# Attention products of two heads on the two halves of TensorE, with results kept feature-major

## The chip, the cores and the metric

One core of a Trainium2 chip runs the whole kernel in one launch. The metric is the device time in microseconds. The engines are TensorE (PE: matrix products; PEld its weight loads), VectorE (DVE), ScalarE (ACT), GpSimd (POOL) and SyncE (SP), whose queue issues nearly all weight transfers. Products land in PSUM, eight banks of 128 x 512 fp32; everything else lives in SBUF.

## What is computed

A chain of transformer blocks on 256 tokens of width 1024, all in fp32. The first block is a gated feed-forward, a mixer (window attention with a context of 256 tokens beside a bidirectional gated scan) and a second feed-forward. A second block follows, twice over, with four token mixers, a gated merge and a mixture of 32 experts. Cut to what the change touches:

```python
s_band = jnp.einsum('bkgnqd,bknsd->bkgnqs', qb, kb).astype(jnp.float32) * scale
...
p = softmax_with_sink(jnp.concatenate([s_band, s_ctx], axis=-1), sink_b).astype(v.dtype)
o = (jnp.einsum('bkgnqs,bknsd->bkgnqd', p[..., :3 * BLOCK], vb)
     + jnp.einsum('bkgnqs,bksd->bkgnqd', p[..., 3 * BLOCK:], vc))
...
o_a = mla_attention(q_nope, q_rope, k_nope, k_rope, v_a).reshape(b, s_len, A_WIDTH)
o_b = stick_breaking_attention(sb[:, :, 0], sb[:, :, 1], sb[:, :, 2]).reshape(b, s_len, B_WIDTH)
o_c = sliding_window_attention(...).reshape(b, s_len, C_WIDTH)
o_d = (rms_norm(o, subln) * (1.0 - lam_init)).reshape(b, s_len, D_WIDTH)
gates = jax.nn.sigmoid(jnp.einsum('bsd,de->bse', x, w_gate) + b_gate).reshape(b, s_len, N_BRANCH, D_MODEL)
merged = (gates[:, :, 0] * jnp.einsum('bsw,wd->bsd', o_a, w_br_a) + ...)
return jnp.einsum('bsd,de->bse', merged, w_out)
```

Heads are 64 wide (differential: scores 32 wide, values 64): eight query heads over two key/value heads in window and sliding-window attention, four heads in the other three.

## The kernel before

Dense products keep fp32 accuracy with three matmuls in fp32r: weights and activations are each cut into a high and a low part, and `mm3` (L149 to L152) adds high x high, high x low and low x high. `Weights` streams 128 x 1024 weight units in a fixed sequence: SP loads a unit into a raw slot, ACT writes the high part (L96), DVE the low part (L97), and a product takes it (`feature_major`, `token_major`). Attention products are plain fp32 matmuls; each stands in the trace as two passes with two records.

PSUM is one pool with two tags of four banks each (`pmm`): "mm" for dense products and "ax" for everything else. Which instruction comes when on each engine is settled when the kernel is built: a scheduler places the instructions of the program in an order on every engine, bound by the buffers that the tiles hold. Tiles of one tag are handed out in program order; a tile gets a buffer when the tile that had it is done with. In the layers all longer-lived tiles share one tag, "u", with 13 buffers (`unit`, L1128):

```python
    def unit(shape, name, dt=FT):
        return U.tile([128] + list(shape), dt, name=name, tag="u", bufs=SHARED)
```

**First block.** `attention(i)` (L825 to L861), for each of two blocks of 128 queries and each of eight heads: scores (L833, one matmul 128 x 512 on 64 rows of the array), mask (L836), maximum (L838 to L840), exp with its sum (L842), four transposes of the probabilities (L845), copy (L847 or L143), four PV products with the probabilities as weights and 64 columns of V streaming (L849), so that the result is token-major; then the division by the sum and four transposes of the result (`rows_T`, L818). It is a generator that yields once per head; `within(i)` is the scan's (L875, L876, L899). L917 to L922 run nine steps of the one with three steps of the other in between. Dense products of the next stage are placed between them by the scheduler.

**A layer** (loop at L1134): projections; sliding-window attention (scores L1254, bias L1257, softmax, transposes L1206, PV L1268); differential attention (scores L1292, bias L1295, maximum L1217, exp L1224, combination L1299 to L1304, PV L1311); stick-breaking (scores L1335 and L1336, L1338 and L1340 on DVE, exp L1341, ln L1342, L1343, suffix products L1345 to L1348, L1349, exp L1350, PV L1356). Exp and ln are in different tables of ACT, and a change of table is an ACT_TABLE_LOAD. Then MLA attention (units `mq`, `mk`; scores L1409, PV L1416) and the gates (32 dense products of 24 matmuls each, for eight units `gt`; tanh at L1428). All five results are token-major, in `OT`, 1280 columns wide; 20 transposes (L1451) turn them into five units `oT` for the merge with the branch weights (L1470 on). Router and experts follow (L1658, L1686); their weights, 192 loads of 512 KB a layer, stream into slots that come free with the attention part.

Of the kernel before, what the change touches and what calls it, by code (L numbers as in the profile page):

```python
# [24 lines left out]
ETB = 2  # L25
QUADS = 8
# [94 lines left out]
def build(tc, A, out):  # L121
# [202 lines left out]
    def gate_rows(pool, i, r, w):  # L324
# [6 lines left out]
        return G  # L331

# [802 lines left out]
    for l in range(2):  # L1135
# [10 lines left out]
        OT = [pL.tile([128, 1280], FT, name=f"o{i}") for i in range(2)]  # L1146
# [93 lines left out]
        project("swk", 1)  # L1240
        for i in range(2):
# [3 lines left out]

            PO = pmm("ax")
            den = pa.tile([128, 8], FT, name="den", bufs=3)
            for s in range(2):
                for g0 in range(0, 4, per):
                    P = pmm("ax")  # L1250
                    Pv = P.rearrange("p (a b) -> p a b", a=per)
                    sc = pa.tile([128, 512], FT, name="sc", bufs=2).rearrange("p (a b) -> p a b", a=per)
                    for j in range(per):
                        PE.matmul(Pv[:, j, :], lhsT=qs["swq"][64 * s:64 * s + 64, g0 + j, qsl],  # L1254
                                  rhs=qs["swk"][64 * s:64 * s + 64, 0, :keys], start=True, stop=True)
                    for j in range(per):
                        V.scalar_tensor_tensor(sc[:, j, :], dist[:, 1, 128 * i:128 * i + keys], -sw_slopes[4 * s + g0 + j],  # L1257
                                               Pv[:, j, :], op0=OP.mult, op1=OP.add)
# [724 lines left out]
```

## Time and profile before

| | |
|---|---|
| median of 3 runs | 2079.13 us (2071.57 to 2079.62) |
| the profiled execution | 2080.24 us, its span 2078.3 us |
| mean granted clock of TensorE | 0.969 |
| PE busy | 1887.0 us, 91% of the span |
| DVE, ACT, POOL busy | 1099.0, 791.3, 244.3 us |
| DMA | 436.61 MB, mean 210 GB/s |

The profile has the share of each engine on one page, and views of the trace give busy time by stretch, by line, and each instruction in order of time. In the timelines "x8" means that eight records in a row were put together; the time given is from the first's start to the last's end, and since matmuls are pipelined, what one costs is read from the start of a row to the start of the next.

### The profile page before, as it was taken

To read this page: it belongs to the slowest core of one execution; us is meant where nothing else is said; L and a number is where in the kernel's file an instruction comes from. 1 tells how busy PE (TensorE), PEld (TensorE's weight loads), DVE (VectorE), ACT (ScalarE), POOL (GpSimd) and SP (SyncE) were. 2 spreads that over 40 slices of the span, in tenths; PEclk is the share of its full clock that TensorE was granted. 3 is DMA by queue.
4 is the path that set the end of the run, shared out by engine and by line. 5 is a ranking of instruction groups with operands and counts; after the bars stand their busy time and mean duration, and the time that the engine had idled before them with its cause. 6 is when DMAs were issued, how large, how long until landed. Compare 5 with 4: busy or idle time off the path is not lost. (4 is left out here: it accounts for less than half of the span.)

```text
span 2078.3 us, 29398 instructions
## 1 busy us (share of the span) xinstructions
PE 1887.0 (91%) x11414; PEld 1447.1 (70%) x11414; DVE 1099.0 (53%) x2083; ACT 791.3 (38%) x1365; POOL 244.3 (12%) x172
## 2 busy tenths in 40 slices
PE   6979999989999897999999997978869999988886
PEld 2757788877778787998888996533238899853331
DVE  4775465484656567554668556211147864641122
ACT  3443222453444444444445644211035465331111
POOL 2653000131131220000100011000020000200000
PEclk9999999999999998999999999999989999989999
DMA  8543575442242134556434378889954445879897
GB/s 317 193 142 122 181 239 198 151 151 87 73 134 81 62 125 131 186 190 191 137 115 138 123 261 313 338 350 412 413 203 133 131 132 177 320 293 412 351 412 283
DMA packets 120118, 436.61 MB, mean 210 GB/s; under 512 B 13616, under 2 KB 13664, under 8 KB 119968
## 3 DMA queue, kind: packets, MB, share of 16 engines
q1 hardware_dynamic: 116208, 422.63, 56.6%
q0 software_dynamic: 2608, 8.32, 1.3%
q10 hardware_dynamic: 1152, 3.67, 0.5%
q8 instruction: 94, 1.54, 0.3%
q14 instruction: 56, 0.46, 0.1%
HBM read 433.51 MB, written 1.05 MB: 209 GB/s over the span
## 5 line engine op out<-in xcount | busy, mean ns | idle before, releaser
L1658 PE MATMUL ax<-raw,xg 128*32 128x512 f32 x1024 | 179.5, 597 | 9.5 <-DMA raw<-in_moe 9.5
L97 DVE TENSOR_TENSOR split7l<-raw,split7h 128x1024 fp32r<-128x1024 f32 x98 | 126.6, 1292 | 112.7 <-ACT split7h L96 112.5
L97 DVE TENSOR_TENSOR split6l<-raw,split6h 128x1024 fp32r<-128x1024 f32 x99 | 128.4, 1297 | 84.4 <-ACT split6h L96 81.5
L96 ACT ACTIVATE split7h<-raw 128x1024 fp32r<-128x1024 f32 x101 | 106.8, 1057 | 169.4 <-PE mm L152 67.0
L96 ACT ACTIVATE split6h<-raw 128x1024 fp32r<-128x1024 f32 x102 | 107.9, 1058 | 161.6 <-issue 59.2
L1658 PEld LDWEIGHTS ax<-raw,xg 128*32 128x32 f32 x1024 | 39.1, 109 | 111.5 <-issue 59.6
L1460 POOL DMA_DIRECT2D gb<-in_lnrows x8 | 4.4, 549 | 835.9 <-DMA raw<-in_moe 416.2
L1686 PE MATMUL ax<-raw,ehT 128*32 128x512 f32 x512 | 87.0, 599 | 15.0 <-ACT ehT L143 12.7
L584 DVE SCALAR_TENSOR_TENSOR xn<-raw,xn 128x1024 f32<-128x1024 f32 x56 | 85.0, 1517 | 23.3 <-DMA raw<-in_w_mod 22.6
L1629 PEld LDWEIGHTS ax<-OH,X 128*128 128x128 f32 x512 | 69.4, 217 | 36.5 <-issue 32.2
L1629 PE MATMUL ax<-OH,X 128*128 128x128 f32 x512 | 75.1, 307 | 13.3 <-issue 11.2
L1691 DVE SCALAR_TENSOR_TENSOR yl<-ax,gsl,yh 128x512 fp32r<-128x512 f32 x32 | 24.0, 751 | 116.1 <-ACT yh L1690 111.7
L581 POOL TENSOR_TENSOR raw<-raw,xn 128x1024 f32<-128x1024 f32 x24 | 72.5, 3030 | 74.8 <-DVE xn L584 56.8
L1667 DVE TENSOR_TENSOR ehs<-ax,ehs 128x256 f32<-128x256 f32 x16 | 6.8, 425 | 119.4 <-ACT ehs L1666 119.4
L361 ACT ACTIVATE xg<-ax,cols 128x128 f32<-128x128 f32 x64 | 24.0, 456 | 117.8 <-PE ax L1629 117.8
L1686 PEld LDWEIGHTS ax<-raw,ehT 128*32 128x32 f32 x512 | 19.3, 108 | 65.4 <-issue 27.6
L1666 ACT ACTIVATE ehs<-ax 128x256 f32<-128x256 f32 x16 | 6.1, 383 | 151.4 <-PE ax L1658 151.4
L363 DVE TENSOR_SCALAR xg<-ax,cols 128x128 f32<-128x128 f32 x64 | 21.9, 405 | 78.0 <-PE ax L1629 78.0
L150 PE MATMUL mm<-hThi,split6h 128*128 128x512 f32 x128 | 52.5, 410 | 6.2 <-ACT split6h L96 4.2
L1690 ACT ACTIVATE yh<-ax,gsl 128x512 fp32r<-128x512 f32 x32 | 21.9, 686 | 94.5 <-PE ax L1686 94.5
L152 PE MATMUL mm<-hThi,split6l 128*128 128x512 f32 x128 | 52.5, 410 | 5.3 <-DVE split6l L97 5.3
L152 PE MATMUL mm<-hxhi,split7l 128*128 128x256 f32 x192 | 54.5, 284 | 2.0 <-POOL split7l L97 1.2
(876 smaller groups left out, 5856.7 us busy)
## 6 DMA issues: line engine op xcount, KB each, us to landing
raw<-in_moe SPq DMA_DIRECT2D x384, 512.0 KB, 10.1
raw<-in_f_in SPq DMA_DIRECT2D x88, 512.0 KB, 4.3
raw<-in_w_gate SPq DMA_DIRECT2D x64, 512.0 KB, 3.5
raw<-in_w_mod SPq DMA_DIRECT2D x56, 512.0 KB, 4.3
raw<-in_f_out SPq DMA_DIRECT2D x55, 512.0 KB, 4.2
raw<-in_w_out SPq DMA_DIRECT2D x24, 512.0 KB, 8.7
raw<-in_w_br SPq DMA_DIRECT2D x20, 512.0 KB, 3.5
raw<-in_w_ada SPq DMA_DIRECT2D x16, 512.0 KB, 9.9
```

What stands on the lines that cost most here:

```text
L96: nc.scalar.activation(hi, x, AF.Copy)
L97: (nc.gpsimd if self.seq[i][1] == "pool" else nc.vector).tensor_tensor(out=lo, in0=x, in1=hi, op=OP.subtract)
L150: PE.matmul(o, lhsT=lh, rhs=rh, start=first, stop=False)
L152: PE.matmul(o, lhsT=ll, rhs=rh, start=False, stop=last)
L361: SC.activation(o, p, AF.Identity, bias=b, scale=g)
L363: V.tensor_scalar(o, p, g, b, op0=OP.mult, op1=OP.add)
L581: GP.tensor_tensor(out=w, in0=w, in1=crow[r], op=OP.mult)
L584: V.scalar_tensor_tensor(mscr, w, 1.0, crow[r], op0=OP.mult, op1=OP.mult, accum_out=m)
L1629: PE.matmul(P[:, 128 * b:128 * b + 128], lhsT=X[:, i, 128 * d:128 * d + 128], rhs=OH[:, i, :], start=i == 0, stop=i == 1)
L1658: PE.matmul(P[32 * s:32 * s + 32, :], lhsT=xg[:, k, 32 * s:32 * s + 32], rhs=ws[s](kk), start=k == 0, stop=k == DT - 1, tile_position=(0, ...
L1686: PE.matmul(P[32 * s:32 * s + 32, :], lhsT=d_["hT"][:, k, 32 * s:32 * s + 32], rhs=ws[s](k), start=k == 0, stop=k == 1, tile_position=(0, ...
L1691: V.scalar_tensor_tensor(yl, P, d_["gsl"], yh, op0=OP.mult, op1=OP.subtract)
```

## The change

Two heads are done as a pair. Their scores are issued one after the other into two "ax" banks: the operands of the two lie on different rows of the array (rows 0 to 63 and 64 to 127, in differential attention neighbouring groups of 32), so that each takes one half. Their PV products swap the operands: 64 columns of V are the weights and the transposed probabilities stream, so that one head's result lands on partitions 0 to 63 and the other's on 64 to 127 of the same bank, feature-major. The division by the sums needs them spread over the columns of that layout: `over_rows` makes this with matmuls of the broadcast reciprocal against the identity, an ACT copy and a DVE product. Results are split into high and low at once and kept in units: two `swo`, `sbo`, `mlo`; only differential attention (which normalizes its rows) stays token-major and is transposed into `dfo`. The transposes of window attention's result and 16 of each layer's 20 go. The units come in program order: `swo` before sliding-window's products, `sbo` after stick-breaking's PV and before `mq` and `mk`, `mlo` before MLA's loop and before the gate tiles. Window attention now has five steps of two heads for six of the scan's. Rows of two weight matrices are put in another order on the host to match. MLA's scores, on 96 rows, stay as they are.

```diff
+    def over_rows(o, p, c, n):
+        R = pmm("ax")
+        for j in range(n):
+            for s in range(2):
+                PE.matmul(R[64 * s:64 * s + 64, 128 * j:128 * j + 128], lhsT=c[:, s, j:j + 1].to_broadcast([128, 64]), rhs=ident,
+                          start=True, stop=True, tile_position=(0, 64 * s))
+        copy_act(o, R[:, :128 * n])
+        V.tensor_tensor(out=o, in0=p, in1=o, op=OP.mult)
...
         for j in range(4):
-            for s in range(2):
-                h = j + 4 * s
-                P = pmm("ax")
+            Ps = [pmm("ax") for _ in range(2)]
+            for s, P in enumerate(Ps):
                 PE.matmul(P, lhsT=aqT[64 * s:64 * s + 64, j, 128 * i:128 * i + 128], rhs=akT[64 * s:64 * s + 64, :],
                           start=True, stop=True)
+            pTs = []
+            for s, P in enumerate(Ps):
+                h = j + 4 * s
...
-                pT = pa.tile([128, 512], FT, name="pT", bufs=2)
+                pT = pa.tile([128, 512], FT, name="pT", bufs=PTB)
                 (V.tensor_copy if h % 2 else copy_act)(pT, PT)
-                for b in range(4):
-                    PE.matmul(PO[:, h * 64:h * 64 + 64], lhsT=pT[:, b * 128:b * 128 + 128], rhs=av[:, b, s * 64:s * 64 + 64],
-                              start=b == 0, stop=b == 3)
-                yield
+                pTs.append(pT)
+            for b in range(4):
+                for s in range(2):
+                    PE.matmul(PO[64 * s:64 * s + 64, 128 * j:128 * j + 128], lhsT=av[:, b, s * 64:s * 64 + 64],
+                              rhs=pTs[s][:, b * 128:b * 128 + 128], start=b == 0, stop=b == 3, tile_position=(0, 64 * s))
+            yield
...
-        V.tensor_tensor(out=o.rearrange("p (h d) -> p h d", h=8), in0=PO.rearrange("p (h d) -> p h d", h=8),
-                        in1=den[:, :, None].to_broadcast([128, 8, 64]), op=OP.mult)
-        rows_T(oaT, i, o)
+        over_rows(o, PO, den.rearrange("p (s j) -> p s j", s=2), 4)
+        sl = slice(128 * i, 128 * i + 128)
+        split(oaT["hi"][:, :, sl], oaT["lo"][:, :, sl], o.rearrange("p (a b) -> p a b", a=4))
...
     for i in range(2):
         a, w = attention(i), within(i)
-        for n in range(9):
+        for n in range(5):
             next(a)
-            for _ in range(3):
+            for _ in range(6):
                 next(w, None)
...
+        swo = [unit([4, 256], "swo", FR) for _ in range(2)]
...
-            for s in range(2):
-                for g0 in range(0, 4, per):
-                    P = pmm("ax")
-                    Pv = P.rearrange("p (a b) -> p a b", a=per)
+            for g0 in range(0, 4, per):
+                Ps = [pmm("ax").rearrange("p (a b) -> p a b", a=per) for _ in range(2)]
+                for j in range(per):
+                    for s in range(2):
+                        PE.matmul(Ps[s][:, j, :], lhsT=qs["swq"][64 * s:64 * s + 64, g0 + j, qsl],
+                                  rhs=qs["swk"][64 * s:64 * s + 64, 0, :keys], start=True, stop=True)
+                Ts = []
+                for s in range(2):
...
-                    T = transposed([pr[:, j, 128 * b:128 * b + 128] for j in range(per) for b in blocks(i)])
-                    for j in range(per):
-                        for b in blocks(i):
-                            PE.matmul(PO[:, 64 * (h0 + j):64 * (h0 + j) + 64], lhsT=T[j * (i + 1) + b],
-                                      rhs=swv[:, b, 64 * s:64 * s + 64], start=b == 0, stop=b == i)
+                    Ts.append(transposed([pr[:, j, 128 * b:128 * b + 128] for j in range(per) for b in blocks(i)]))
+                for j in range(per):
+                    for b in blocks(i):
+                        for s in range(2):
+                            PE.matmul(PO[64 * s:64 * s + 64, 128 * (g0 + j):128 * (g0 + j) + 128], lhsT=swv[:, b, 64 * s:64 * s + 64],
+                                      rhs=Ts[s][j * (i + 1) + b], start=b == 0, stop=b == i, tile_position=(0, 64 * s))
             V.reciprocal(den, den)
-            V.tensor_tensor(out=OT[i][:, 512:1024].rearrange("p (h d) -> p h d", h=8), in0=PO.rearrange("p (h d) -> p h d", h=8),
-                            in1=den[:, :, None].to_broadcast([128, 8, 64]), op=OP.mult)
+            o = pa.tile([128, 512], FT, name="sc", bufs=2)
+            over_rows(o, PO, den.rearrange("p (s j) -> p s j", s=2), 4)
+            split(swo[0][:, :, qsl], swo[1][:, :, qsl], o.rearrange("p (a b) -> p a b", a=4))
...
             for g0 in range(4):
-                n = 2
-                o = 32 * g0
-                P = pmm("ax")
-                Pv = P[:, :2 * keys].rearrange("p (a b) -> p a b", a=n)
+                if g0 % 2 == 0:
+                    for g in (g0, g0 + 1):
+                        Ps[g] = pmm("ax")[:, :2 * keys].rearrange("p (a b) -> p a b", a=n)
+                    for j in range(n):
+                        for g in (g0, g0 + 1):
+                            o = 32 * g
+                            PE.matmul(Ps[g][:, j, :], lhsT=qs["dfq"][o:o + 32, j, qsl], rhs=qs["dfk"][o:o + 32, j, :keys],
+                                      start=True, stop=True, tile_position=(o, 0))
+                Pv = Ps.pop(g0)
...
+        Pz = {}
         for h in range(4):
-            o = 64 * (h % 2)
-            q_, k_ = qs["sbq"][o:o + 64, h // 2, :], qs["sbk"][o:o + 64, h // 2, :]
-            P = pmm("ax")
-            PE.matmul(P[:, 0:256], lhsT=k_[:, 0:128], rhs=q_, start=True, stop=True)
-            PE.matmul(P[:, 256:384], lhsT=k_[:, 128:256], rhs=q_[:, 128:256], start=True, stop=True)
+            if h % 2 == 0:
+                for hh in (h, h + 1):
+                    Pz[hh] = pmm("ax")
+                for kc, qc, n in ((0, 0, 256), (128, 128, 128)):
+                    for hh in (h, h + 1):
+                        o = 64 * (hh % 2)
+                        q_, k_ = qs["sbq"][o:o + 64, hh // 2, :], qs["sbk"][o:o + 64, hh // 2, :]
+                        c = 2 * kc
+                        PE.matmul(Pz[hh][:, c:c + n], lhsT=k_[:, kc:kc + 128], rhs=q_[:, qc:qc + n], start=True, stop=True)
+            P = Pz.pop(h)
...
-        for i in range(2):
-            PO = pmm("ax")
-            for h in range(4):
+        PO = pmm("ax")
+        for p in range(2):
+            for i in range(2):
                 for b in blocks(i):
-                    PE.matmul(PO[:, 64 * h:64 * h + 64], lhsT=aTs[h][:, 128 * (i + b):128 * (i + b) + 128],
-                              rhs=vv[:, b, 64 * h:64 * h + 64], start=b == 0, stop=b == i)
-            V.tensor_copy(OT[i][:, 256:512], PO[:, :256])
+                    for s in range(2):
+                        h = 2 * p + s
+                        PE.matmul(PO[64 * s:64 * s + 64, 256 * p + 128 * i:256 * p + 128 * i + 128],
+                                  lhsT=vv[:, b, 64 * h:64 * h + 64], rhs=aTs[h][:, 128 * (i + b):128 * (i + b) + 128],
+                                  start=b == 0, stop=b == i, tile_position=(0, 64 * s))
+        sbo = unit([2, 2, 256], "sbo", FR)
+        split(sbo[:, 0], sbo[:, 1], PO.rearrange("p (a b) -> p a b", a=2))
         mq, mk = unit([4, 256], "mq"), unit([4, 256], "mk")
...
+        mlo = unit([2, 2, 256], "mlo", FR)
...
-                for j in range(per):
+                for j in range(0, per, 2):
                     for b in blocks(i):
-                        PE.matmul(PO[:, 64 * (g0 + j):64 * (g0 + j) + 64], lhsT=T[j * (i + 1) + b],
-                                  rhs=mv[:, b, 64 * (g0 + j):64 * (g0 + j) + 64], start=b == 0, stop=b == i)
+                        for s in range(2):
+                            h = g0 + j + s
+                            PE.matmul(PO[64 * s:64 * s + 64, 64 * (g0 + j):64 * (g0 + j) + 128], lhsT=mv[:, b, 64 * h:64 * h + 64],
+                                      rhs=T[(j + s) * (i + 1) + b], start=b == 0, stop=b == i, tile_position=(0, 64 * s))
...
+            o = pa.tile([128, 512], FT, name="sc", bufs=2)[:, :256]
+            over_rows(o, PO[:, :256], den[:, 0:4].rearrange("p (j s) -> p s j", s=2), 2)
+            split(mlo[:, 0, :, qsl], mlo[:, 1, :, qsl], o.rearrange("p (a b) -> p a b", a=2))
...
-        oT = [unit([2, 2, 256], "oT", FR) for _ in range(5)]
-        for k in range(0, 10, 2):
-            P = pmm("ax")
-            for kk in range(2):
-                for i in range(2):
-                    c = (k + kk) * 128
-                    PE.transpose(P[:, kk * 256 + i * 128:kk * 256 + i * 128 + 128], OT[i][:, c:c + 128], ident)
-            split(oT[k // 2][:, 0], oT[k // 2][:, 1], P.rearrange("p (a b) -> p a b", a=2))
+        dfo = unit([2, 2, 256], "dfo", FR)
+        P = pmm("ax")
+        for kk in range(2):
+            for i in range(2):
+                PE.transpose(P[:, kk * 256 + i * 128:kk * 256 + i * 128 + 128], OT[i][:, 128 * kk:128 * kk + 128], ident)
+        split(dfo[:, 0], dfo[:, 1], P.rearrange("p (a b) -> p a b", a=2))
+        def oT(k):
+            if 4 <= k < 8:
+                return [w[:, k - 4, :] for w in swo]
+            w = {0: mlo, 1: sbo, 4: dfo}[k // 2]
+            return [w[:, n, k % 2, :] for n in range(2)]
...
```

Below, lines of the changed kernel from L335 on lie higher than before's: L1365 are stick-breaking's scores, L1375 to L1378 the suffix products, L1388 the PV products, L1335 differential PV, L1224 transposes, L1314 differential scores, L147 the high part of a result, L1466 the gates.

Before, on PE, the end of one stick-breaking head and the start of the next:

```order
L150 MATMUL mm<-xhi_7879,split6h 128x256
L151 MATMUL mm<-xlo_7881,split6h 128x256
L1345 MATMUL ax<-sbe,m_6275 128x128
L1346 MATMUL ax<-sbe,m_6275 128x128
L1347 MATMUL ax<-sbe,m_6275 128x128
L1348 MATMUL ax<-sbe,m_6275 128x128
L1335 MATMUL ax<-sbqk 128x256
L1336 MATMUL ax<-sbqk 128x128
L152 MATMUL mm<-xhi_7879,split6l 128x256
L150 MATMUL mm<-xhi_7880,split6h 128x256
```

The suffix products of a head stand between dense products of the gates (`xhi`, `xlo` are the layer's input); from the scores of one head to its suffix products there are 52, 51, 48 and 48 dense rows for the four heads.

The change, on PE, from the last dense product in differential attention (its `cT` are the MLA projections) to the first stick-breaking scores:

```order
L153 MATMUL mm<-cThi,split22l 128x256
L1335 MATMUL ax<-vv,pT 128x64 x2
L1224 MATMUL ax<-ident,pr 128x128 x2
L1314 MATMUL ax<-dfqk 128x256 x2
L1335 MATMUL ax<-vv,pT 128x64 x2
L1314 MATMUL ax<-dfqk 128x256 x2
L1224 MATMUL ax<-ident,pr 128x128 x4
L1335 MATMUL ax<-vv,pT 128x64 x2
L1365 MATMUL ax<-sbqk 128x256
L1335 MATMUL ax<-vv,pT 128x64 x2
L1365 MATMUL ax<-sbqk 128x256
L1365 MATMUL ax<-sbqk 128x128 x2
```

The heads of a pair now follow each other, transposes and PV of differential attention run straight into stick-breaking, and the next dense product after the first of these rows stands behind the 12 PV products of stick-breaking, 30 rows on.

The change, on ACT, from the second pair of stick-breaking heads to the copies of the MLA projections (`sbe`, `sbz`: the exponentials and scores of stick-breaking):

```order
L1371 ACTIVATE sbe<-sbe 128x384 x2
L1372 ACT_TABLE_LOAD
L1372 ACTIVATE sbe<-sbe 128x384 x2
L1380 ACT_TABLE_LOAD
L1380 ACTIVATE sbz<-sbz 128x384 x2
L147 ACTIVATE sbo<-ax 128x512
L144 ACTIVATE mq<-mm 64x512 x2
L144 ACTIVATE mv<-mm 128x512
L97 ACTIVATE split22h<-raw_9361 128x1024
```

`sbo` is written first, then `mq` and `mv`, then weights are split again; the first gate row (L1466) comes seven rows behind the last of these. Before, gate rows and weight splits stood between the stick-breaking rows on ACT too.

## Rows read from the trace of the kernel before

**Rows 1.** The page, part 1: busy time, share, instructions.
```profile
PE 1887.0 (91%) x11414; PEld 1447.1 (70%) x11414; DVE 1099.0 (53%) x2083; ACT 791.3 (38%) x1365; POOL 244.3 (12%) x172
```
**Rows 2.** Busy time by stretch: window attention, sliding-window and differential, stick-breaking, experts.
```profile
core 0: us, PE busy (x) PEld busy (x) DVE busy (x) ACT busy (x) POOL busy (x), PEclk, DMA share, GB/s
586.00:733.00 147.00, 137.52 (x878) 112.25 (x877) 88.60 (x151) 61.84 (x116) 41.83 (x41) 0.98 0.27 88
...
1076.00:1135.00 59.00, 56.67 (x423) 51.53 (x422) 47.87 (x108) 30.54 (x67) 0.00 (x0) 1.00 0.42 134
1135.00:1171.00 36.00, 35.25 (x280) 33.61 (x280) 22.17 (x43) 27.78 (x37) 0.00 (x0) 1.00 0.42 132
...
1300.00:1530.00 230.00, 193.51 (x1152) 80.91 (x1152) 46.99 (x133) 39.74 (x85) 5.78 (x4) 0.96 0.95 378
```
**Rows 3.** Timeline of SP's queue, first layer: first load of expert weights.
```profile
1227.61 0.33 SPq L79 DMA_DIRECT2D raw<-in_moe  x1
```
**Rows 4.** The page, costliest groups: busy time, mean ns of one.
```profile
L1658 PE MATMUL ax<-raw,xg 128*32 128x512 f32 x1024 | 179.5, 597 | 9.5 <-DMA raw<-in_moe 9.5
```
**Rows 5.** Timeline of PE in window attention: start us, us, line, operation.
```profile
643.75 1.12 PE L833 MATMUL ax<-akT,aqT 64*128 64x512 f32 x2
644.80 0.39 PE L152 MATMUL mm<-hxhi,split7l 128*128 128x256 f32 x1
```
**Rows 6.** Timeline of PE in stick-breaking, first layer.
```profile
1133.58 0.70 PE L1335 MATMUL ax<-sbqk 64*128 64x256 f32 x2
1134.11 0.38 PE L1336 MATMUL ax<-sbqk 64*128 64x128 f32 x2
1134.42 0.66 PE L1311 MATMUL ax<-vv,pT 128*128 128x64 f32 x4
...
1166.03 0.46 PE L1345 MATMUL ax<-sbe,m 128*128 128x128 f32 x2 [0.17 <-DVE sbe L1343]
...
1167.00 2.12 PE L1356 MATMUL ax<-vv,sbz 128*128 128x64 f32 x18
1168.96 0.89 PE L1409 MATMUL ax<-mk,mq 96*128 96x128 f32 x6
```
**Rows 7.** Timeline of PE at the transposes of the results, first layer.
```profile
1218.58 1.91 PE L1451 MATMUL ax<-ident,o 128*128 128x128 f32 x16
1220.62 0.38 PE L150 MATMUL mm<-oT,split7h 128*128 128x256 f32 x1
```
**Rows 8.** Timeline of PE in sliding-window attention, first layer.
```profile
1045.59 0.70 PE L1254 MATMUL ax<-swk,swq 64*128 64x256 f32 x2
1046.21 0.33 PE L1206 MATMUL ax<-ident,pr 128*128 128x128 f32 x1
```
**Rows 9.** Timeline of DVE in stick-breaking: the first of a head's four passes.
```profile
1135.88 0.55 DVE L1338 SCALAR_TENSOR_TENSOR sbz<-ax,m 128x384 f32<-128x384 f32 x1
```
**Rows 10.** Timeline of ACT in stick-breaking, first head.
```profile
1137.26 0.53 ACT L1341 ACTIVATE sbe<-sbe 128x384 f32<-128x384 f32 x1 [1.75 <-DVE sbe L1340]
...
1138.75 1.28 ACT L1342 ACT_TABLE_LOAD   x1
1140.04 0.53 ACT L1342 ACTIVATE sbe<-sbe 128x384 f32<-128x384 f32 x1
```
**Rows 11.** Timelines of DVE and ACT, last differential head of the first layer.
```profile
1127.07 0.74 DVE L1295 SCALAR_TENSOR_TENSOR sc<-dist,ax 128x256 f32<-128x256 f32 x2
...
1132.67 0.48 DVE L1304 SCALAR_TENSOR_TENSOR pr<-pr,dend 128x256 f32<-128x256 f32 x1
...
1130.62 0.49 ACT L1224 ACTIVATE pr<-sc,mx 128x256 f32<-128x256 f32 x1
1131.02 0.19 ACT L1224 ACTIVATION_READ_ACCUMULATOR pr<-sc,mx 128x1 f32 x1
```
**Rows 12.** Busy time by stretch, in the router of the first layer (columns as in rows 2).
```profile
1294.00:1303.00 9.00, 4.18 (x19) 4.13 (x20) 5.59 (x26) 2.44 (x5) 0.00 (x0) 0.50 0.76 308
```
**Rows 13.** Line L845, its engine sat idle before it (us, times) until:
```profile
  ACT pr L842: 13.8, 14
```

More of the change, by code (lines that the diff above doesn't have):

```diff
@@ L25 @@
 ETB = 2
+PTB = 2
 QUADS = 8
@@ L1145, in build @@
         xt2 = [(xT, 0), (xT, 1)]
-        OT = [pL.tile([128, 1280], FT, name=f"o{i}") for i in range(2)]
+        OT = [pL.tile([128, 256], FT, name=f"o{i}") for i in range(2)]
         at = ExitStack()
@@ L1247, in build @@
             den = pa.tile([128, 8], FT, name="den", bufs=3)
-            for s in range(2):
-                for g0 in range(0, 4, per):
-                    P = pmm("ax")
-                    Pv = P.rearrange("p (a b) -> p a b", a=per)
+            for g0 in range(0, 4, per):
[6 more added lines that the diff above has]
+                for s in range(2):
                     sc = pa.tile([128, 512], FT, name="sc", bufs=2).rearrange("p (a b) -> p a b", a=per)
                     for j in range(per):
-                        PE.matmul(Pv[:, j, :], lhsT=qs["swq"][64 * s:64 * s + 64, g0 + j, qsl],
-                                  rhs=qs["swk"][64 * s:64 * s + 64, 0, :keys], start=True, stop=True)
-                    for j in range(per):
                         V.scalar_tensor_tensor(sc[:, j, :], dist[:, 1, 128 * i:128 * i + keys], -sw_slopes[4 * s + g0 + j],
-                                               Pv[:, j, :], op0=OP.mult, op1=OP.add)
+                                               Ps[s][:, j, :], op0=OP.mult, op1=OP.add)
                     h0 = 4 * s + g0
@@ L1284, in build @@
             PO = pmm("ax")
+            n = 2
+            Ps = {}
             for g0 in range(4):
-                n = 2
-                o = 32 * g0
-                P = pmm("ax")
-                Pv = P[:, :2 * keys].rearrange("p (a b) -> p a b", a=n)
+                if g0 % 2 == 0:
[7 more added lines that the diff above has]
+                Pv = Ps.pop(g0)
                 sc = pa.tile([128, 512], FT, name="sc", bufs=2)[:, :2 * keys].rearrange("p (a b) -> p a b", a=n)
-                for j in range(n):
-                    PE.matmul(Pv[:, j, :], lhsT=qs["dfq"][o:o + 32, j, qsl], rhs=qs["dfk"][o:o + 32, j, :keys],
-                              start=True, stop=True, tile_position=(o, 0))
                 for j in range(n):
@@ L1312, in build @@
                                   start=b == 0, stop=b == i)
-            od = OT[i][:, 1024:1280]
+            od = OT[i]
             copy_act(od, PO[:, :256])
@@ L1413, in build @@
                 T = transposed([pr[:, j, 128 * b:128 * b + 128] for j in range(per) for b in blocks(i)])
-                for j in range(per):
+                for j in range(0, per, 2):
                     for b in blocks(i):
-                        PE.matmul(PO[:, 64 * (g0 + j):64 * (g0 + j) + 64], lhsT=T[j * (i + 1) + b],
-                                  rhs=mv[:, b, 64 * (g0 + j):64 * (g0 + j) + 64], start=b == 0, stop=b == i)
+                        for s in range(2):
+                            h = g0 + j + s
+                            PE.matmul(PO[64 * s:64 * s + 64, 64 * (g0 + j):64 * (g0 + j) + 128], lhsT=mv[:, b, 64 * h:64 * h + 64],
+                                      rhs=T[(j + s) * (i + 1) + b], start=b == 0, stop=b == i, tile_position=(0, 64 * s))
             V.reciprocal(den[:, :4], den[:, :4])
-            V.tensor_tensor(out=OT[i][:, 0:256].rearrange("p (h d) -> p h d", h=4), in0=PO[:, :256].rearrange("p (h d) -> p h d", h=4),
-                            in1=den[:, 0:4, None].to_broadcast([128, 4, 64]), op=OP.mult)
+            o = pa.tile([128, 512], FT, name="sc", bufs=2)[:, :256]
+            over_rows(o, PO[:, :256], den[:, 0:4].rearrange("p (j s) -> p s j", s=2), 2)
+            split(mlo[:, 0, :, qsl], mlo[:, 1, :, qsl], o.rearrange("p (a b) -> p a b", a=2))
         gts = []
@@ L1487, in build @@
                 mm3(P[b // 2][:, 256 * (b % 2):256 * (b % 2) + 256], wb[0][:, c:c + 128], wb[1][:, c:c + 128],
[L1488 removed]
+                    *oT(k), kk == 0, kk == n_in[b] - 1)
                 blk += 1
@@ L1873, in layout @@
         o[n] = mov(p[n])
-    for n, z in (("w_oa", I["w_o_attn"][0]), ("w_oh", I["w_o_hgrn"][0])):
+    w_oa = I["w_o_attn"][0].reshape(2, 4, 64, D).transpose(1, 0, 2, 3).reshape(512, D)
+    for n, z in (("w_oa", w_oa), ("w_oh", I["w_o_hgrn"][0])):
         o[n] = np.ascontiguousarray(stat(z).reshape(4, 2, 128, 512).transpose(0, 2, 1, 3)).reshape(4, 128, 1024)
@@ L1955, in layout @@
         gate.append(g)
-        b = np.concatenate([J["w_br_" + n][l] for n in "abcd"], 0)
+        b = {n: J["w_br_" + n][l] for n in "abcd"}
+        b["c"] = b["c"].reshape(2, 4, 64, D).transpose(1, 0, 2, 3).reshape(512, D)
+        b = np.concatenate([b[n] for n in "abcd"], 0)
         b = b.reshape(10, 128, DT, 128).transpose(2, 0, 1, 3).reshape(10, 8, 128, 128).transpose(0, 2, 1, 3)
```

1 line of the change is left out of this document (removed).

## The prediction, made before the change was run

> **What bounds the kernel now.** I read the page's busy shares first, then busy time by stretches, then the waits of single lines, then timelines. TensorE is busy for 91% of the span [rows 1], so work taken off it can show, but only where it is what ends last. The stretches separate two regimes [rows 2]. In the three that the change touches (window attention from 586 us; sliding-window and differential products; stick-breaking) PE is busy for 137.5 of 147, 56.7 of 59 and 35.3 of 36 us: PE-bound, with dense products filling the gaps that the softmax chains leave. In 1300:1530, the experts, the DMA share is 0.95: weights bound it. Their first load starts at 1227.61 us [rows 3], after gates and merge have begun, and waits for the pools of the attention part to be freed; so a microsecond won or lost in attention moves the experts by a microsecond. Nothing behind it gives it back.
>
> **What is saved on PE.** An fp32 matmul is two passes (two records). I take what lies between the starts of rows, not their durations, which overlap. That small column tiles run side by side is seen in before: 1024 passes of L1658, of mean 597 ns, make only 179.5 us of busy time [rows 4]; one after another they would make about 600. So I let a pair of heads cost what one costs.
> - Window attention: 16 score matmuls at 1.05 us [rows 5] make 16.8, halved: -8.4. The 128 passes of its PV products at 0.109 us (18 passes between 1167.00 and 1168.96 [rows 6]) make 14.0, halved: -7.0. Eight transposes of the result go, at 0.128 (16 between 1218.58 and 1220.62 [rows 7]): -1.0. The new `over_rows` adds 16 matmuls, 32 passes in pairs, 16 x 0.121 (eight 128-column passes between 1166.03 and 1167.00 [rows 6]): +1.9. Sum **-14.5**.
> - Each layer: sliding-window scores, 8 matmuls of 256 columns at 0.31 each (two passes; row "x2" from 1045.59 to 1046.21 is 0.62 for one matmul [rows 8], which I take for one 256-column matmul, and 0.31 for a 128-column one from 1134.11 to 1134.42 [rows 6]): 8 x 0.62 + 8 x 0.31 = 7.4, halved -3.7. Differential scores have the same shapes on 32 rows: -3.7. Stick-breaking: 4 x 0.84 (1133.58 to 1134.42) = 3.4, halved -1.7. PV: 48 + 24 + 24 passes x 0.109 = 10.5, halved -5.2. 16 transposes fewer: -2.0. `over_rows`, 24 pairs x 0.121: +2.9. Sum **-13.4**.
>
> ACT copies and splits of the results change places more than number; they lie beside PE's work, except where named below. The permuted weight rows are made on the host and cost nothing.
>
> **What becomes late.** The order shows where the price lies. The shared units are handed out in program order. The result unit of stick-breaking, `sbo`, now stands before `mq`, `mk` and the gate tiles `gt`, and all come from one ring of 13. So the gates' dense products, which in before fill 52, 51, 48 and 48 rows between one head's scores and its suffix product, now come after stick-breaking's PV; from the middle of the second differential block to that PV, PE has not one dense product. What covered these chains is gone, and they are paid for in full:
> - Stick-breaking, per layer. VectorE's four passes a head take about 0.55 us each [rows 9], ACT's 0.53 and a table load 1.28 [rows 10]. First pair: two DVE passes 1.1; on ACT exp, load, ln, load, exp, load, ln = 4 x 0.53 + 3 x 1.28 = 6.0; DVE 0.55; suffix products 0.97; DVE 0.55: 9.1. Second pair: three DVE passes 1.65; exp twice 1.06; load 1.28; ln twice 1.06; DVE 0.55, products 0.97, DVE 0.55, exp 0.53: 7.65. PV 12 x 0.121 = 1.45. That is 18.2; with handoffs I take 19.5. PE's own work in it is 1.7 + 3.9 + 1.45 = 7.05, so **+12.5**.
> - Second differential block: its last two heads run on DVE and ACT as one chain: three bias passes 3 x 0.37 and a maximum of about two such; four exps with their sums, 4 x 0.68 (0.49 and 0.19); the combination of the last head about 1.15, of which 0.48 has a row [rows 11]; then transposes, copy and PV 1.3: 7 to 8.5 us with some 2 us of PE work. With the first pair, which has little cover left, I take **+6.5**. First block: +1.
> - Sliding window: two softmax chains now end together and the second head's transposes wait for it, some 2 us at two of the four pairs: +3.5.
> - Resuming: the dense products need PSUM banks that hold the MLA projections until `sbo` and the `mq`, `mk` copies are written, ACT 3 to 4 passes of 0.5 to 0.6: +3, and +1 in MLA.
> - Clock: where PE worked 4.18 of 9 us the granted clock was 0.50, the lower level (1.2 GHz) [rows 12]. A stretch of about 30 us with 10 us of PE work comes into being in each layer; bounds 0 and +9, since its work and the first products after it can cost double. I take +3: only part of the stretch is so empty.
> Sum +30.5, less the idle time that before has in the same stretches, 2.3 + 0.8 [rows 2]: +27.4. **Net per layer +14.**
>
> Window attention also pays: transposes already wait 13.8 us for ACT [rows 13]; two heads of a pair now go through DVE in turn, and eight pairs at about 1.3 us are 10, to which come the first and last pair. By the order, dense products now last to its end (184 follow the scan's last product, 50 before), so I charge no more than +2.5: **-12** (-17 to -6).
>
> **Sum.** -12 + 2 x 14 = +16 on the profiled execution's 2080.24 us: 2096. The median of the runs shown is 1.1 lower, so in its terms **2095**.
>
> The row on the largest term shows the ACT instruction behind a table load starting 1.29 us after the load did [rows 10]. The Trainium skill (ScalarE: Activation LUTs, What ACT_TABLE_LOAD costs) puts every switch of a set at 2.66 us, the load and a drain behind it; by it six loads a layer would add 8.3 us each time and give 2112. This trace has the 1.28 us and no drain behind it, so I give that case no chance of its own.
>
> **The rivals.**
> - *The hold is cheap (faster, 2060).* The mechanism of the forecast is the waiting chain of differential and stick-breaking products; if its handoffs overlap better than I chain them (second pair's DVE passes beside the first pair's table loads), it costs a third: 10 instead of 27 a layer, less than the pairing saves. Then the time is 2080 - 12 - 2 x 4 = 2060. It decides below 13 us of stall a layer. For it: DVE is free there. Against it: the order has the second pair's DVE passes behind the first pair's last one. Chance 0.22.
> - *It comes out even (2080).* Stalls of 19.5 a layer: -12 + 2 x 6 = 0. Chance 0.26.
> - *Score pairs don't run side by side (2121).* The row tiles of two heads write to two banks; before has no two neighbouring matmuls on different rows, only on different columns [rows 4]. Without it 8.4 + 2 x 9.1 = 26.6 us of the saving go: 2095 + 26 = 2121. Chance 0.10. The Trainium skill (TensorE: Matmul & The Clock Gate, Part 3) reports 3.07x for four row tiles, which speaks against this rival; no run here shows it.
> - *Forecast*: 2095, in itself 2086 to 2110, chance 0.42.
>
> **How the numbers follow.** A measurement can tell 0.5% of 2079, 10.4 us, from no change: faster is below 2068.7, slower above 2089.5. Faster 0.22; same 0.26; slower 0.42 + 0.10 = 0.52. Cases of both signs count, so the range reaches from inside the first rival to just short of the last: 2060 to 2117, which leaves out about 0.1 at either end.
>
> **What would show it.** Right: between the last differential scores and stick-breaking's PV no dense product on PE, PE busy about a third there, 25 to 35 us long, in both layers; the first gate activation (L1428 of before) starts after the last stick-breaking exp; the first expert load about 14 us later than now relative to window attention's end; pairs of PV and score passes starting within some 10 ns; window attention's stretch about 12 us shorter. Wrong: gate products among the stick-breaking rows, or a stretch below 20 us (first rival); the passes of score pairs one after another at about 0.3 us (last rival); a granted clock of 1.00 through the hold would take my +3 back.

## The result: 0.94% slower, and the profile after

The changed kernel takes 2097.37 us in the median (2091.74 to 2098.51, 4 runs) against 2079.38 (2071.57 to 2081.61, 4 runs): a ratio of 1.0094 (95% interval 1.0078 to 1.0111). The forecast was 2095, slower by more than 0.5%. The profiled execution of the change is the shortest of its four, 2091.74 us, 11.5 above the profiled execution of before; durations below come from it. That execution of before, 2080.24 us, is itself 2.6 to 5.7 us longer than the medians of before that stand beside the experiments (2077.65, 2077.03 and 2074.59), so a gain read from stretches against it can be too large by as much; the ratios are free of this.

PE has less to do and the kernel is longer. The page, part 1, after (busy time, share, instructions), beside [rows 1]:

```profile
PE 1866.9 (89%) x11502; PEld 1430.2 (68%) x11502; DVE 1082.5 (52%) x2081; ACT 792.8 (38%) x1373; POOL 244.3 (12%) x172
```

Busy time by stretch, first layer, after (columns as in [rows 2]): sliding window, the differential blocks, their end, stick-breaking, the resumption, and what follows.

```profile
1014.00:1050.00 36.00, 35.81 (x274) 28.74 (x273) 26.04 (x66) 21.30 (x56) 0.00 (x0) 1.00 0.36 118
1050.00:1081.00 31.00, 28.78 (x217) 25.33 (x217) 24.57 (x79) 14.68 (x38) 0.00 (x0) 0.99 0.41 136
1081.00:1089.00 8.00, 2.82 (x13) 1.56 (x11) 5.47 (x17) 2.46 (x9) 0.00 (x0) 0.50 0.01 4
1089.00:1113.00 24.00, 13.19 (x53) 10.83 (x52) 10.61 (x31) 13.67 (x18) 0.00 (x0) 0.57 0.00 0
1113.00:1121.00 8.00, 5.07 (x38) 4.82 (x38) 6.71 (x10) 3.26 (x6) 0.00 (x0) 0.71 0.00 0
...
1146.00:1220.00 74.00, 74.00 (x625) 74.00 (x625) 30.97 (x26) 36.24 (x53) 2.28 (x4) 1.00 0.57 187
```

From 1081 to 1121 us PE is busy for 21.1 of 40 us, at half clock for most of it, and even the DMA queues stand still (share 0.01 and 0.00); no weights are consumed there. In [rows 2] the same products ran in stretches that were busy for 92 of 95 us at full clock. Behind it, from 1146 to 1220, PE does without a gap what it had done between the heads before.

The timeline of PE in that stretch, after (start, us, line; in brackets the idle time ahead and who ended it): the last pair of differential scores, the heads behind it, and stick-breaking.

```profile
1080.56 1.22 PE L1314 MATMUL ax<-dfqk 32*128 32x256 f32 x4
1086.53 0.66 PE L1224 MATMUL ax<-ident,pr 128*128 128x128 f32 x2 [4.75 <-DVE dend L1323]
...
1090.15 1.11 PE L1335 MATMUL ax<-vv,pT 128*128 128x64 f32 x4
1091.19 1.65 PE L1365 MATMUL ax<-sbqk 64*128 64x256 f32 x6
1096.89 0.77 PE L1375 MATMUL ax<-sbe,m 128*128 128x128 f32 x2 [4.06 <-issue]
...
1100.52 0.80 PE L1375 MATMUL ax<-sbe,m 128*128 128x128 f32 x2 [1.58 <-DVE sbe L1373]
...
1109.35 0.77 PE L1375 MATMUL ax<-sbe,m 128*128 128x128 f32 x2 [5.17 <-DVE sbe L1373]
...
1111.19 0.63 PE L1375 MATMUL ax<-sbe,m 128*128 128x128 f32 x2
...
1113.04 2.19 PE L1388 MATMUL ax<-sbz,vv 128*64 128x128 f32 x24
1118.16 0.55 PE L151 MATMUL mm<-split22h,cThi 128*128 128x256 f32 x1 [2.93 <-DVE rt L1414]
```

Not one dense product stands between the last differential heads and 1118.16. The same holds in the second layer: no dense product in 32 us. Eight passes of suffix products take 1.84 us (1109.35 to 1111.19) where [rows 6] has 0.97.

What the pairs save is there too. Sliding-window scores of eight heads, after, and what follows them:

```profile
1014.35 1.16 PE L1270 MATMUL ax<-swk,swq 64*128 64x128 f32 x16
1015.44 0.50 PE L151 MATMUL mm<-split7h,xhi 128*128 128x512 f32 x1
```

16 passes in 1.09 us; issued one head at a time, 8 passes take as long (below).

Three stretches make the balance. Each is the time between first starts of lines on PE: window attention's first scores to the layers' first scores (L833 to L1254 of before), and in each layer from there to the first expert product (L1658). For all kernels of this study, from their profiled executions, in us:

| kernel | window attention to layers | first layer | second layer |
|---|---|---|---|
| before | 445.4 | 274.1 | 272.4 |
| the change | 429.8 | 289.0 | 288.5 |
| own tiles | 429.1 | 267.2 | 268.5 |
| only sbo its own | 432.9 | 290.5 | 290.0 |
| window attention alone | 433.2 | 272.1 | 271.0 |
| hold alone | 443.1 | 323.9 | 325.9 |
| units created early | 433.1 | 289.0 | 288.4 |
| units written early | 432.2 | 267.7 | 268.5 |
| differential scores single | 428.4 | 266.2 | 265.9 |
| all scores single | 436.6 | 273.4 | 273.5 |
| score pairs only | 432.1 | 267.6 | 269.5 |
| hold filled | 432.2 | 286.9 | 286.0 |

The change wins 15.6 us in the first stretch and loses 14.9 and 16.1 in the layers. These make +15.4, and the profiled execution is 11.5 longer; the other 4 us lie outside the three stretches, where nothing was changed. Kernels with the same window attention as the change lie between 428.4 and 433.2 in the first column, and those with the same layers within 2 us: readings scatter by 5 us in the first column and by 2 in the others.

### The profile page after: what moved, and what is told of

The parts are those of the page before. It is cut to its first block, busy times and chain, and to the rows that moved or that the text cites. A ratio compares the mean times of both kernels' runs of the same rounds, so it can differ in the third digit from the quotient of the medians.

```text
span 2089.7 us, 29613 instructions
## 1 busy us (share of the span) xinstructions
PE 1866.9 (89%) x11502; PEld 1430.2 (68%) x11502; DVE 1082.5 (52%) x2081; ACT 792.8 (38%) x1373; POOL 244.3 (12%) x172
```

## The experiments

The theory: the new result units keep the dense products behind them, and the softmax chains that lose this cover are paid for in full. The main rival: pairing itself costs, since chains of two heads end together.

**Own tiles.** The two units leave the ring; nothing else is changed.

```diff
-        sbo = unit([2, 2, 256], "sbo", FR)
+        sbo = pL.tile([128, 2, 2, 256], FR, name="sbo")
...
-        mlo = unit([2, 2, 256], "mlo", FR)
+        mlo = pL.tile([128, 2, 2, 256], FR, name="mlo")
```

> The changed kernel, with the result tiles sbo and mlo taken from the layer's own pool and no longer from the ring of 13 units. Theory (dense products are held back behind sbo and mlo in the ring): the gates' products stand between the stick-breaking rows again, the hold of some 35 us a layer is gone, the granted clock there is 1.00, and of the pairing the saving remains: window attention -16 and each layer -8 to -13 against before, so 2079 - 16 - 2 x 10 = 2043 (2036 to 2055). Rival (pairing itself costs what was seen: softmax chains of two heads ending together, more changes of tile layout): no better than about 2085.

2056.40 us (5 runs) against 2074.59 of before beside it, a ratio of 0.9915 (0.9901 to 0.9928). Differential attention, stick-breaking and MLA in this kernel, by stretch:

```profile
1055.00:1103.00 48.00, 44.05 (x306) 39.05 (x304) 39.88 (x108) 22.33 (x55) 0.00 (x0) 0.89 0.30 99
1103.00:1128.00 25.00, 22.92 (x194) 20.86 (x190) 16.73 (x38) 20.62 (x30) 0.00 (x0) 1.00 0.41 130
1128.00:1148.00 20.00, 20.00 (x170) 18.20 (x170) 11.97 (x21) 11.15 (x29) 0.00 (x0) 1.00 0.38 125
```

Stick-breaking is busy for 22.9 of 25 us at a clock of 1.00. A layer is 20 to 22 us shorter than in the change: that is the price of the hold, and the pairs stay. The total is 18 us below before where 36 were expected, just outside the range, and the first row shows where to look: the differential stretch has idle time and a clock of 0.89.

**Only sbo its own.** 

> The changed kernel, with sbo alone taken from the layer's own pool; mlo still comes from the ring before the gate tiles. Theory: only the MLA projections may now fill the stick-breaking chain, some 70 dense products of 0.118 us, 8 us a layer, while the gates wait for mlo and MLA's chain is left uncovered in part: 2097 - 2 x 8 = 2081 (2065 to 2095), with the gates' first activation behind MLA's first result. Rival (sbo alone holds everything): as fast as with both tiles out of the ring, about 2043.

2102.85 us in one run: the hold is not shortened at all. `mlo`, still in the ring, holds the gates just as long:

```profile
1103.00:1127.00 24.00, 14.02 (x92) 12.50 (x91) 13.37 (x35) 15.62 (x21) 0.00 (x0) 0.72 0.28 89
1127.00:1152.00 25.00, 20.09 (x125) 15.86 (x122) 8.18 (x17) 9.14 (x28) 0.00 (x0) 0.73 0.03 6
```

Stick-breaking is busy for 14 of 24 us, and now MLA's stretch stalls too. The projections that came free went ahead of it, into the differential stretch, which is 48 us long as with both tiles out. Both the theory and the rival missed: that freeing dense work helps in proportion to its amount was wrong; it has to be there when the chain needs it.

**Hold alone.** Before, nothing paired, with one more unit in the ring; its content is never read.

```diff
+        hold = unit([2, 2, 256], "hold", FR)
+        for i in range(2):
+            V.tensor_copy(hold[:, 0, i, :], SBP[i][:, :256])
         mq, mk = unit([4, 256], "mq"), unit([4, 256], "mk")
```

> Before, with nothing paired, and one more unit of the ring written from stick-breaking's results before mq and mk (it is not read). Theory: the dense products leave the stick-breaking rows as in the change; four heads one after another of about 7 us each lie open, with differential attention's end some 25 to 30 us of stall a layer, and half clock in it: 2079 + 2 x 27 = 2133 (2115 to 2155). Rival (the place of a unit in the ring doesn't matter, the pairs make the stall): within 5 us of before.

2182.01 us in one run: 50 and 53 us a layer, twice the expectation. A unit nobody reads costs 5%. Where it went:

```profile
1104.00:1129.00 25.00, 11.85 (x31) 6.87 (x31) 9.07 (x26) 3.66 (x13) 0.00 (x0) 0.50 0.00 0
1129.00:1166.00 37.00, 19.30 (x77) 16.05 (x76) 12.69 (x34) 18.26 (x24) 0.00 (x0) 0.53 0.00 1
```

Four single heads of stick-breaking take 37 us with no dense product among them, no less than with 199 of them in between before; I had counted only the end of the differential stretch, which lies open for 25 us with PE busy under half, and too little for what half clock does to PE's own work. With pairs the hold is less than half as dear: 20 to 22 against 50 to 53.

**Window attention alone**, by the change's edits there. 

> Before, with the window attention of the first block alone changed (pairs, over_rows, five steps of six). Theory: the stretch from its first scores to the layers' first scores is about 16 us shorter and the rest is as before: 2079 - 16 = 2063 (2060 to 2068). Rival (the gain there is an effect of the order of the whole and not of the pairs): 2075 or more.

2066.67 (8 runs) against 2074.59: ratio 0.9964 (0.9949 to 0.9978), 7.9 us. The first stretch is 12.2 shorter, the layers are within 2 of before. The time lies in the expected range, but the gain is half of the 16 that were expected. Those were read from the change's trace alone, against the one profile of before; this stretch gives 12 to 17 over all kernels that have pairs of scores in it, and the total, which does not hang on that profile, is the better measure.

**Units created early, and units written early.** Which property of a unit makes it hold? In the first kernel `sbo` and `mlo` are created beside `swo`; in the second they are also written there, one column each:

```diff
+        sbo, mlo = (unit([2, 2, 256], n, FR) for n in ("sbo", "mlo"))
+        for w in (sbo, mlo):
+            V.tensor_copy(w[:, 0, 0, 0:1], lam[:, 0:1])
...
-        sbo = unit([2, 2, 256], "sbo", FR)
...
-        mlo = unit([2, 2, 256], "mlo", FR)
```

> The changed kernel, with sbo and mlo created (as tiles of the ring) already beside swo, ahead of sliding-window's products; they are first written where they were. The hold of the dense products is certain by now; open is what of a unit makes it. Theory A (units get their buffers in the order in which the program first writes them): nothing changes, 2097 (2088 to 2106), no dense product between the stick-breaking rows. Theory B, as the prediction put it (in the order in which the program creates them): the hold is gone, as with tiles of their own, about 2056.

> As the run before this, and one column of sbo and of mlo is written right after they are created, by two tiny copies on VectorE (overwritten later). Theory A (order of first writes): the hold is gone, 2056 (2050 to 2062), granted clock 1.00 in the stick-breaking stretch. Theory B or any that puts it on the ring's size: as the change, about 2097.

Created early: 2096.95 us in one run, the change's time, and layers of 289.0 and 288.4. Written early: 2059.58 us (4 runs; ratio 0.9905, 0.9879 to 0.9931), with stick-breaking at full clock:

```profile
1106.00:1131.00 25.00, 22.91 (x193) 21.03 (x192) 16.70 (x37) 20.71 (x30) 0.00 (x0) 1.00 0.40 130
```

So the place of creation doesn't matter, nor that two more units share the ring: the units come into use in the order in which the program first writes them, and one that is written late keeps all behind it waiting. Two copies of one column undo the loss.

**Differential scores single**, on top of own tiles. The 2.6 us that PE waits there between two heads of a pair, with the clock at 0.71 and 0.79 in the 21 us from 1082 on, is what was left over:

```profile
1081.53 0.66 PE L1335 MATMUL ax<-vv,pT 128*128 128x64 f32 x4
1084.80 0.44 PE L1224 MATMUL ax<-ident,pr 128*128 128x128 f32 x2 [2.61 <-DVE pr L1328]
```

```diff
-                if g0 % 2 == 0:
-                    for g in (g0, g0 + 1):
-                        Ps[g] = pmm("ax")[:, :2 * keys].rearrange("p (a b) -> p a b", a=n)
-                    for j in range(n):
-                        for g in (g0, g0 + 1):
-                            o = 32 * g
+                for g in (g0,):
+                    Ps[g] = pmm("ax")[:, :2 * keys].rearrange("p (a b) -> p a b", a=n)
+                    for j in range(n):
+                        o = 32 * g
```

> The kernel with sbo and mlo as tiles of their own, with differential scores issued one head at a time again. In that kernel the differential stretch has PE busy 44.1 of 48 us and a granted clock of 0.89, since the second head's transposes come right behind the first's and wait for its softmax. Theory (pairing the scores makes the two chains end together and costs more there than the 3.7 us of PE work that it saves a layer): 2056 - 2 x 3 = 2050 (2044 to 2057), that stretch at a clock of 1.00. Rival (the stall has another cause): 2056 + 2 x 3.7 = 2063.

2050.78 us (4 runs) against 2077.65: ratio 0.9873 (0.9857 to 0.9890), the fastest of all kernels here and 2.2% below the change. Its layers are 1.0 and 2.6 us shorter than with own tiles alone; of the 6.8 us between the two profiled executions 3.7 lie ahead of window attention, where nothing was changed. The differential stretch is longer, 63 us, but filled, and at full clock:

```profile
1051.00:1114.00 63.00, 60.59 (x453) 54.97 (x451) 49.69 (x114) 32.20 (x69) 0.00 (x0) 1.00 0.42 140
1114.00:1138.00 24.00, 21.99 (x184) 20.03 (x182) 16.47 (x37) 19.61 (x28) 0.00 (x0) 1.00 0.31 99
```

**All scores single**, PV products still in pairs. 

> The same, with all score products of window, sliding-window, differential and stick-breaking attention issued one head at a time; PV products stay in pairs. Theory: PE work of 8.4 in window attention and 5.4 a layer comes back on top of the run before this one, about 19, of which perhaps 5 is won back from chains that no longer end together: 2050 + 14 = 2064 (2056 to 2072). Rival (pairs of scores save nothing): within 4 us of the run before.

2074.24 us (10 runs): ratio 0.9985 (0.9970 to 1.0001) to before, 23 us above the run before this one where 14 were expected: nothing was won back. The first stretch is 8.2 longer, the layers 7.2 and 7.6. The sliding-window scores show it; four heads now take the 1.09 us that eight took:

```profile
1026.12 1.16 PE L1270 MATMUL ax<-swk,swq 64*128 64x128 f32 x8
1027.21 0.50 PE L151 MATMUL mm<-split7h,xhi 128*128 128x512 f32 x1
```

**Score pairs only**: window attention as in the change, and in the layers only the scores of sliding-window and stick-breaking attention in pairs. 

> Before, with window attention as in the change, and in the layers only the scores of sliding-window and stick-breaking attention in pairs; the layers' PV products, transposes and result tiles are as before, so no new unit stands in the ring. The profiles so far put a layer at 274.1 and 272.4 us before, 266 with pairs of scores and of PV (differential scores single) and 273.5 with pairs of PV alone. Theory (in the layers it is the score pairs that pay, and the PV pairs with their over_rows give nothing): 2051 to 2057 on a chip where before is 2077. Rival (PV pairs are worth the 4 us of PE work that the prediction counted, hidden in the last run by something else): 2059 to 2063.

2057.98 us (4 runs): ratio 0.9906 (0.9884 to 0.9927), between the two theories. Its layers are 1.4 and 3.6 us longer than with PV pairs, while PV pairs without score pairs gave 0.7 and -1.1 against before. What the PV pairs are worth in a layer's time, between nothing and 4 us, stays open. On PE, adding up what lies between the starts of rows (first layer, before and differential scores single), the PV products that are paired went from 10.7 us to 7.6, the transposes that go took 1.9 and `over_rows` takes 3.2: 1.8 us less in all.

**Hold filled.** The change, with products that nobody reads where PE waits in the hold:

```diff
+            for _ in range(12 if h % 2 == 0 else 4):
+                PE.matmul(P[:, 384:512], lhsT=tri, rhs=z[:, 0:128], start=True, stop=True)
             PE.matmul(P[:, 0:128], lhsT=tri, rhs=e[:, 0:128], start=True, stop=True)
```

> The change, with matmuls of no use put into the hold: ahead of the suffix products of each pair's first head 12, of its second head 4, from the biased scores into a corner of the same PSUM bank that nothing reads (2.9 and 1.0 us at the full clock, where PE waits 4 and 1.6 us). Theory (the hold is also paid in half clock: eight passes of suffix products take 1.86 us there where they take 0.97 at the full clock): with PE kept busy the granted clock in the hold rises above 0.8, the products on the chain are 3 to 4 us shorter a layer and the total is 2097 - 6 = 2091 (2086 to 2096). Rival (the clock doesn't come back within the hold, or isn't on the chain): the useless passes run at half clock, 5.2 us, overrun the wait and cost 2 to 6 us: 2099 to 2106.

2092.68 us (4 runs): ratio 1.0070 (1.0045 to 1.0095), against the change's 1.0094; the intervals overlap, so the total shows a gain only weakly. The layers are 2.1 and 2.5 us shorter, where the change and units created early, with the same layers, agree to 0.1. The trace shows why:

```profile
1092.00:1118.00 26.00, 20.87 (x143) 18.17 (x143) 13.48 (x35) 16.09 (x23) 0.00 (x0) 0.83 0.00 1
...
1101.37 0.39 PE L1377 MATMUL ax<-sbe,m 128*128 128x128 f32 x2
...
1102.26 1.06 PE L1376 MATMUL ax<-sbz,m 128*128 128x128 f32 x8
```

The clock is 0.83 where it was 0.57, and eight passes of suffix products take 0.89 us (L1377 is their first line here, L1376 the filling). The first filling of 24 passes still ran at half clock (4.7 us), so not all of it was won.

## Why the prediction was right, and where it was not

- **The mechanism** (dense products held back behind the new units; differential end and stick-breaking laid bare) is shown from both sides: taking the units out of the ring, or writing one column of them early, ends it; adding a unit to before brings it. The signs came as named: 32 us in each layer without a dense product, the first gate activation (1133.52) behind the last stick-breaking exp (1113.73), and the first expert load 17.9 us later than before, counted from the first sliding-window scores. PE is busy for half of those 32 us, not a third, since half clock draws its work out. The step's reason was off by one word: not the order of creation but of first writes.
- **Stick-breaking**, 19.5 us with 3 us a layer for the clock: from the first DVE pass at 1092.46 to the PV products' end at 1115.23 it takes 22.8, and filled it is 2.6 shorter. Right, as was resuming (2.93 us of idle time at 1118.16, 3 predicted). An instruction behind a table load starts 1.29 us after it (1094.39 to 1095.68), as in [rows 10], so the longer switch that would have given 2112 is not there.

```profile
1092.46 0.56 DVE L1368 SCALAR_TENSOR_TENSOR sbz<-ax,m 128x384 f32<-128x384 f32 x1 [0.33 <-PE ax L1365]
```

- **Differential end**: from the last scores at 1080.56 to the last PV row's end at 1091.26 it is 10.7 us, not 7 to 8.5; half clock (0.50) runs through all of it, and I had priced the clock only once for the whole hold.
- **Sliding window, +3.5**: wrong. PE is busy for 35.81 of 36 us there; the dense products cover the second head.
- **Window attention, -12**: 12.2 to 17 by the stretch, 7.9 by the total of window attention alone (interval 4.6 to 10.6). Near enough, but both of its parts were too large. By the starts of rows PE saves 10.3 us there, not 14.5: scores 7.1 (8.4 predicted), PV products 4.3 (7.0), transposes 0.9, less 2.1 for `over_rows`. And the +2.5 of stall did not come: PE is idle for 23.7 us of the stretch against 25.2, and the transposes (L861 after) wait for ACT half as long as in [rows 13] (us, times):

```profile
  ACT pr L858: 6.9, 14
```

- **The saving of a layer, -13.4**, was counted too high, and the rows say where. Sliding-window and stick-breaking scores save 3.5 and 1.5 us of PE (3.7 and 1.7 predicted). PV products save 3.0, not 5.2. A pair streams 128 columns of probabilities where a single pass streamed 64 of V, and it was priced at one such pass; eight single passes took 0.81 us before, 0.10 each, and seven pairs take 1.02 after, 0.15 each:

```profile
1067.91 1.00 PE L1268 MATMUL ax<-swv,pT 128*128 128x64 f32 x8
1068.72 0.37 PE L152 MATMUL mm<-xhi,split6l 128*128 128x256 f32 x1
...
1044.63 1.09 PE L1288 MATMUL ax<-pT,swv 128*64 128x128 f32 x14
1045.65 0.39 PE L152 MATMUL mm<-xlo,split7h 128*128 128x256 f32 x1
```

- Differential scores save 1.3 to 1.8, not 3.7 (7.0 us a layer one head at a time, 5.2 and 5.7 in pairs in own tiles). There the passes of a pair do not all lie beside each other: other rows stand between them, and six passes take as long as four of one head did before. The chain of the pair costs more than that saving: without this pair the layers are 1.0 and 2.6 shorter, the first of which is within the scatter.

```profile
1112.62 1.13 PE L1292 MATMUL ax<-dfqk 32*128 32x256 f32 x4
1113.68 0.38 PE L152 MATMUL mm<-xhi,split7l 128*128 128x256 f32 x1
...
1070.49 0.69 PE L1314 MATMUL ax<-dfqk 32*128 32x256 f32 x2
1071.12 0.43 PE L1335 MATMUL ax<-vv,pT 128*128 128x64 f32 x2
1071.48 1.12 PE L1314 MATMUL ax<-dfqk 32*128 32x256 f32 x6
1072.54 0.39 PE L153 MATMUL mm<-xhi,split22l 128*128 128x256 f32 x1
```

- **So two errors met, and that the net of +14 came out is in part luck.** The saving is some 8 us a layer, not 13.4: 6.7 without the differential pair by the rows above (transposes and `over_rows` with them), where the layers of differential scores single are 7.9 and 6.5 shorter than before's, and 1.3 to 1.8 for that pair. With the 14.9 and 16.1 that the layers lost, the stalls are then 23 to 24, not 27.4; sliding window's 3.5, which are none, are nearly all of the difference. Of the stalls 20 to 22 are the hold, measured between the change and own tiles; the rest can be laid to the differential pair's chain, which stays without the hold. With the saving as predicted and these stalls a layer would have lost 10, and the sum would have been near 2087 (-12 + 2 x 10), which the prediction counts as no change.
- **The rivals.** The cheap hold would have been 10 us a layer and the even case 19.5; the stalls are 23 to 24. Score pairs do run side by side: the passes of two heads start 7 ns apart as a rule, sliding-window scores take 3.5 us a layer where they took 7.0, and issuing all scores singly costs 8.2 us in window attention's stretch (8.4 predicted, in readings that scatter by 5).

## What to carry to other kernels

Before tiles are added to a shared ring, see where in the program each is first written: one that is written at the end of a long chain keeps back the work that hides this chain, and neither its size nor its use shows it. When two heads are made a pair, their chains end together; that pays where products are long and other work lies beside them (window attention, sliding window), and not where the chain itself is the limit (differential attention). Where a pair swaps its operands, count the columns that then stream; half of what streamed before is not the price. And a saving on the busiest engine should be counted with the order of the new program in hand, for what covers each wait may have moved.

## What was not expected of the hardware

Work of no use shortened a layer by 2 us: with PE kept busy, the granted clock in the hold rose from 0.57 to 0.83, and eight passes of suffix products went from 1.84 us to 0.89. Pairs of scores with 512 columns don't always cost the same: four passes took 1.06 us in one place and 1.34 in another, with nothing waited for in between (the row ahead, the pair, the row behind):

```profile
583.96 0.66 PE L808 MATMUL ax<-ident,s 128*128 128x128 f32 x4
584.55 1.13 PE L846 MATMUL ax<-akT,aqT 64*128 64x512 f32 x4
585.61 0.50 PE L152 MATMUL mm<-split7l,hxhi 128*128 128x512 f32 x1
...
601.03 0.40 PE L894 MATMUL ax<-Mh,lfl 128*128 128x512 f32 x1
601.36 1.41 PE L846 MATMUL ax<-akT,aqT 64*128 64x512 f32 x4
602.70 0.51 PE L152 MATMUL mm<-split7l,hxhi 128*128 128x512 f32 x1
```

In all nine kernels with these pairs it is the same four of the eight: those right behind a 512-column product of the scan (L894), where the second head's first pass starts 0.29 to 0.37 us after the first head's. In the four behind a 128-column product it starts 7 ns after. Whether the row ahead is the cause is not shown, since place and row ahead never change separately; it accounts for the 1.3 us by which these pairs save less than predicted.
